# VectorE adds in place of adding DMAs in the first part of each FFN, and one group with three pairs in seven products instead of four

## The chip, the cores and the metric

The kernel runs on one core of a Trainium2 chip. The metric is the device time of one execution in microseconds. Three runs of the kernel before gave 2097.92, 2096.4 and 2097.1 us, median 2097.1. The profile is of one further execution.

## The reference

A trunk of two residual layers over 256 tokens of width 2048 in fp32. Each layer has a mixer (layer 0: sliding window attention beside a matrix memory; layer 1: forgetting attention) and an FFN of hidden width 5632. The change lies in the FFN:

```python
def swiglu(xn, w_gate, w_up, w_down):
    return (jax.nn.silu(xn @ w_gate) * (xn @ w_up)) @ w_down

# per layer, after the mixer
h = h + swiglu(rms_norm(h, norm_ffn[layer]), w_gate[layer], w_up[layer], w_down[layer])
```

## The kernel before

**Products.** An fp32 operand is split into a high and a low part in a reduced format: ScalarE casts the raw tile to `hi` (L187, L356), VectorE computes `lo = raw - hi` (L188, L357). A product of two split operands is three matmuls into one accumulator, hi·xh (L532), lo·xh (L533) and hi·xl (L534); the helper `three` issues them. The two token tiles of 128 are the stationary side, 512 columns of weights the moving side.

**Stages of an FFN.** The hidden width is cut into 11 groups of 512 columns, numbered 0 to 10, in three parts: groups 0 to 2, 3 to 6 and 7 to 10. Each part first does its groups (gate and up columns of the same number together, then SiLU and multiplication, then a turn of the result by DMA transposes on SyncE's queue and `join`, which splits it for the next product), and then two calls for `w_down`, each for 1024 output columns.

**Pairs of rows.** Every such call is a `pair_group` (L539). It walks over the contraction in pairs of 128 rows; a gate and up group has eight pairs. A plain pair (kind 0) does eight products, 24 matmuls. A mixed pair (kind 1) does seven products, 21 matmuls, after the scheme of Strassen and Winograd: `ra` and `rb` are two raw tiles of 128 x 2 x 512 (gate and up, or two column blocks of `w_down`), loaded by SyncE's DMA queue, 512 KB each. Sums of weight blocks are formed in place and split again:

1. `rb[:,0] += ra[:,0]`, before the change by a DMA that GpSimd issues: it reads those 256 KB of gate (or down) rows from HBM once more and adds them onto `rb` (L599).
2. `ra` is split (L187, L188), and the sum `rb` is split as `hu`, `lu` (L356, L357).
3. `rb[:,1] = rb[:,0] - rb[:,1]` on VectorE, 128x512 (L605), then `ra -= rb[:,1]`, 128x1024 (L607), and both results are split again (L356, L357).

`combine` (from L552) puts the products together after the last mixed pair.

**Which pairs are mixed.** `ORDER` makes three of eight pairs mixed (1, 3 and 5) and starts with a plain one; `HEAVY` makes four mixed (1, 3, 5, 7) and starts with a mixed one. `DENSE` lists the groups that take `HEAVY`. In the down products of the first part two of six pairs are mixed, in the other parts three of eight (`DOWN`).

**Order and buffers.** A scheduler fixes the order of each engine's stream when the kernel is built, and each engine then runs its stream in that order. Raw tiles of mixed pairs come from a pool of five buffers, those of plain pairs from another of four; a load can start when the instruction that last read its buffer is done. The `w_in_even` and `w_in_odd` projections use `pair_group` too, in a variant (`halves`) that has no adding DMA.

Of the kernel before, what the change touches and what calls it, by code (L numbers as in the profile page):

```python
# [12 lines left out]
ALU = mybir.AluOpType  # L13
# [10 lines left out]
NB = 512  # L24
# [11 lines left out]
ORDER = ((0, 0), (1, 1), (0, 2), (1, 3), (0, 4), (1, 5), (0, 6), (0, 7))  # L36
HEAVY = ((1, 1), (0, 0), (1, 3), (0, 2), (1, 5), (0, 4), (1, 7), (0, 6))
FOURTH = 7
DENSE = (1, 4, 5, 8, 9)
DOWN = {  # L40
    6: ((0, 0), (1, 1), (0, 2), (1, 3), (0, 4), (0, 5)),
    8: ((0, 0), (1, 1), (0, 2), (1, 3), (0, 4), (1, 5), (0, 6), (0, 7)),
# [33 lines left out]
def trunk(  # L76
# [19 lines left out]
    nc = tc.nc  # L96
# [58 lines left out]
    for n in (1, 2, 3):  # L155
# [8 lines left out]
        out=ident, in_=ident, pattern=[[-1, P]], compare_op=ALU.not_equal, fill=1.0, base=0, channel_multiplier=1  # L164
# [73 lines left out]
    sums = {}  # L238
# [116 lines left out]
    def split_plain(dst_h, dst_l, src):  # L355
        nc.scalar.copy(dst_h, src)  # L356
        nc.vector.tensor_tensor(out=dst_l, in0=src, in1=dst_h.bitcast(F32), op=ALU.subtract)  # L357
# [178 lines left out]
    def bank(par, name):  # L536
        return pm.tile([P, NB], F32, tag="pm", name=name) if par else pa.tile([P, NB], F32, tag="acc", name=name)

    def pair_group(fp, par, lhs, sums, mats, order, todo=(), halves=None, inner=None, raws=None):  # L539
        plain = [[bank(par, "acc") for _ in range(NT)] for _ in range(2)]  # L540
        begun = set()

        def fresh(*at):
            known = at in begun
            begun.add(at)
            return not known

        todo = list(todo)
        prods = None
        kinds = [kind for kind, _ in order]  # L550
        t0, t1 = slice(0, P), slice(P, 2 * P)

        def combine(prods):
            c = fp.tile([P, 4, NB], F32, tag="c", name="c", bufs=1)
            nc.scalar.copy(c[:, 0, :], prods[0])
            if halves is None:
                nc.vector.tensor_tensor(out=c[:, 1, :], in0=prods[3], in1=c[:, 0, :], op=ALU.add)
                nc.vector.tensor_tensor(out=c[:, 2, :], in0=prods[2], in1=c[:, 1, :], op=ALU.add)
                nc.vector.tensor_tensor(
                    out=c[:, 1:4:2, :],  # L560
                    in0=prods[1].rearrange("p (a n) -> p a n", a=1).broadcast_to([P, 2, NB]),
                    in1=c[:, 1:3, :],
                    op=ALU.subtract,
                )
                return c
            nc.vector.tensor_tensor(out=c[:, 2, :], in0=prods[3], in1=c[:, 0, :], op=ALU.add)
            nc.vector.tensor_tensor(out=c[:, 1, :], in0=prods[2], in1=c[:, 2, :], op=ALU.add)
            nc.vector.tensor_tensor(out=c[:, 3, :], in0=prods[1], in1=c[:, 1, :], op=ALU.subtract)
            nc.vector.tensor_tensor(out=c[:, 2, :], in0=prods[1], in1=c[:, 2, :], op=ALU.subtract)
            return c  # L570

        for pos, (kind, pair) in enumerate(order):
            k0 = 2 * pair
            if inner is not None and pos == len(order) - 1:
                c = combine(prods)
                inner()
            if not kind:
                last = pos == len(order) - 1
                walk = [(i, t) for i in range(CK) for t in range(NT)]
                if last:  # L580
                    walk.sort(key=lambda it: it[1])
                for m, (w, c0) in enumerate(mats):
                    hi, lo = load_chunk(w, k0, c0, NB)
                    run_due(todo, pos)
                    for i, t in walk:
                        ah, al = lhs(k0 + i)
                        ts = slice(t * P, (t + 1) * P)
                        three(
                            plain[m][t], ah[:, ts], al[:, ts], hi[:, i, :], lo[:, i, :],
                            fresh(m, t), last and i == CK - 1,  # L590
                        )
                continue
            first, last = 1 not in kinds[:pos], 1 not in kinds[pos + 1 :]
            if first:
                prods = [bank(1 - par, "prod") for _ in range(4)]
            ra, rb = (load_raw(w, k0, c0, NB, fp, W_RAWS if halves else RAWS, raws) for w, c0 in mats)
            if halves is None:
                (w, c0), part = mats[0], slice(k0 * P, (k0 + 1) * P)
                nc.gpsimd.dma_start(rb[:, 0, :], w[part, c0 : c0 + NB], accum_op=ALU.add)  # L599
            hg, lg = split_chunk(ra, NB)  # L600
            run_due(todo, pos)
            hu, lu = slot()
            if halves is None:
                split_plain(hu, lu, rb)
                nc.vector.tensor_tensor(out=rb[:, 1, :], in0=rb[:, 0, :], in1=rb[:, 1, :], op=ALU.subtract)  # L605
                both = rb[:, 1, :].rearrange("p (a n) -> p a n", a=1).broadcast_to([P, CK, NB])
                nc.vector.tensor_tensor(out=ra, in0=ra, in1=both, op=ALU.subtract)  # L607
                hc, lc = (a[:, 0, :] for a in slot())
                split_plain(hc, lc, rb[:, 1, :])
                hd, ld = slot()  # L610
                split_plain(hd, ld, ra)
                ht = [hu[:, 0, :], hd[:, 0, :], hc, hd[:, 1, :]]
                lt = [lu[:, 0, :], ld[:, 0, :], lc, ld[:, 1, :]]
            else:
                split_plain(hu[:, 1, :], lu[:, 1, :], rb[:, 1, :])
                nc.vector.tensor_tensor(out=ra[:, 0, :], in0=rb[:, 0, :], in1=ra[:, 0, :], op=ALU.add)
                nc.vector.tensor_tensor(out=rb[:, 0, :], in0=rb[:, 1, :], in1=rb[:, 0, :], op=ALU.subtract)
                nc.vector.tensor_tensor(out=rb[:, 1, :], in0=ra[:, 0, :], in1=rb[:, 1, :], op=ALU.subtract)
                nc.vector.tensor_tensor(out=ra[:, 1, :], in0=ra[:, 1, :], in1=rb[:, 1, :], op=ALU.subtract)
                parts = []  # L620
                for src in (ra, rb):
                    hs, ls = halves.pop(0)
                    halves.append((hs, ls))
                    split_plain(hs, ls, src)
                    parts.append((hs, ls))
                where = ((0, 0), (1, 0), (1, 1), (0, 1))
                ht = [parts[a][0][:, b, :] for a, b in where]
                lt = [parts[a][1][:, b, :] for a, b in where]
            sh, sl = sums(pair)
            xa, la = lhs(k0)  # L630
            xb, lb = lhs(k0 + 1)
            three(prods[0], xa[:, t0], la[:, t0], hg[:, 0, :], lg[:, 0, :], first, last)
            three(plain[0][0], xb[:, t0], lb[:, t0], hg[:, 1, :], lg[:, 1, :], fresh(0, 0), False)
            three(plain[1][0], sh[3], sl[3], hu[:, 1, :], lu[:, 1, :], fresh(1, 0), False)
            three(prods[1], sh[0], sl[0], ht[0], lt[0], first, last)
            three(prods[2], sh[2], sl[2], ht[1], lt[1], first, last)
            three(prods[3], sh[1], sl[1], ht[2], lt[2], first, last)
            three(plain[0][1], xb[:, t1], lb[:, t1], ht[3], lt[3], fresh(0, 1), False)
        if inner is None:
            c = combine(prods)  # L640
        return plain, c

    def ffn(layer, fp, sx, x4, sd, key, todo, idx_next=None, key_next=None, finish=None):
# [8 lines left out]
        for g0, g1 in zip(PARTS, PARTS[1:]):  # L652
            end = g1 == PARTS[-1]
            nk = 4 * (g1 - g0)
            order = DOWN[nk // 2]
            for g in range(g0, g1):
                par = (g1 - 1 - g) % 2
# [5 lines left out]
                    [(w_gate[layer], g * NB), (w_up[layer], g * NB)],  # L663
                    HEAVY if g in DENSE else ORDER,
                    todo,
                )
                todo = []
                for m in range(2):
# [79 lines left out]
            for n0 in (0, 2):  # L748
                if end and idx_next is None and n0 == 2:
                    for n in (2, 3):  # L750
                        acc = new_acc()
                        gemm(acc, m_of, wd, n * NB, NB, 0, nk, nk, skew=3 if n == 3 else 1, halved=n == 3)
                        close(acc, n)
                    continue
                plain, c = pair_group(
                    fp, 1 - n0 // 2, m_of, sums_d, [(wd, n0 * NB), (wd, (n0 + 1) * NB)], order, todo
                )
                todo = []
                if end and idx_next is None:
                    gf = fp.tile([P, D], F32, tag="c", name="gf", bufs=1)  # L760
                    nc.gpsimd.dma_start(gf, norm_final.partition_broadcast(P))
                for t in range(NT):
                    o = h[:, t, n0 * NB : (n0 + 2) * NB]
                    nc.vector.tensor_tensor(
                        out=o, in0=c[:, 2 * t : 2 * t + 2, :].rearrange("p a n -> p (a n)"), in1=o, op=ALU.add
                    )
                for m in range(2):
                    close(plain[m], n0 + m)
# [614 lines left out]
```

## Time and profile before

| | |
|---|---|
| median of three runs | 2097.1 us |
| profiled execution, its own time | 2095.33 us |
| its span, first to last instruction | 2093.6 us |
| matmuls on TensorE | 9443 |
| adding DMAs on GpSimd (L599) | 76 of 256 KB |
| first part of the FFN, layer 0 and 1 | from about 290 to 497 and from about 1360 to 1565 us of the span |

The page of the profile gives busy time by engine, a row of 40 slices, the chain of work that ended last, and groups of instructions. The trace itself answers closer questions: a windows view (busy time of each engine in a stretch of time), timelines of one engine with what ended each idle time, and lists of waits. PE is TensorE's matmuls, PEld its weight loads, DVE VectorE, ACT ScalarE, POOL GpSimd, SP SyncE. A row such as `lo<-raw,hi` names what an instruction writes and reads. Times in the timelines count from the start of the span.

### The profile page before, as it was taken

How to read it: one execution, taken by the hardware profiler on the slowest of the kernel's cores; microseconds unless marked ns; L12 is line 12 of the kernel's file. 1: busy time of each engine (PE TensorE's matmuls, PEld its weight loads, DVE VectorE, ACT ScalarE, POOL GpSimd, SP SyncE). 2: the span in 40 equal slices, each digit the busy share in tenths (PEclk: the TensorE clock that was granted, in tenths of full speed). 3: DMA queues.
4: the chain of work that ended last, by engine and by line, in shares of the span. 5: the costliest groups of instructions: out<-in, count | busy, mean ns of one | idle time of the engine just before them, and what ended most of it. 6: DMA issues, size and time to landing. Idle time of an engine off the chain costs nothing.

```text
span 2093.6 us, 27094 instructions
## 1 busy us (share of the span) xinstructions
PE 2072.1 (99%) x9443; PEld 1709.8 (82%) x9443; DVE 1794.4 (86%) x2217; ACT 1384.1 (66%) x1764; POOL 133.7 (6%) x171
## 2 busy tenths in 40 slices
PE   9999999999999999999999999999999999999998
PEld 8878887778888888888888888887788888888887
DVE  6788768988999998998899678578899999999995
ACT  6767677665567656667676776686655667557763
POOL 1010000000000000000000001000000000000000
PEclk9999999999999999999999999999999999999999
DMA  8666578777788777887676777597778777867864
GB/s 294 177 201 201 195 257 226 217 215 218 220 229 265 227 244 220 237 238 202 204 225 198 227 201 186 162 263 202 243 220 244 228 223 234 265 201 209 263 208 150
DMA packets 324698, 462.43 MB, mean 221 GB/s; under 512 B 108092, under 2 KB 116304, under 8 KB 324432
## 3 DMA queue, kind: packets, MB, share of 16 engines
q1 hardware_dynamic: 307088, 426.27, 64.8%
q0 software_dynamic: 16752, 33.33, 9.0%
q8 instruction: 74, 1.21, 0.2%
q10 hardware_dynamic: 720, 1.09, 0.1%
q14 instruction: 64, 0.52, 0.1%
HBM read 436.21 MB, written 2.12 MB: 209 GB/s over the span
## 4 chain that ended last, share of the span: by engine, by line
PE 75%; DVE 8%; DMA 6%; ACT 5%; issue 4%; SPq 0%; ACTq 0%; POOLq 0%; POOL 0%; DVEq 0%
PE acc L533 16%; PE acc L532 16%; PE acc L534 16%; PE prod L533 4%; PE prod L532 4%; PE prod L534 4%; PE acc L222 4%; PE acc L223 4%; PE acc L224 4%; DVE lo L188 2%; DVE lo L357 2%; DMA raw<-in_w_down_dram 2%; ACT hi L187 2%; DMA raw<-in_w_gate_dram 1%; ACT hi L356 1%
## 5 line engine op out<-in xcount | busy, mean ns | idle before, releaser
L188 DVE TENSOR_TENSOR lo<-raw,hi 128x1024 fp32r<-128x1024 f32 (+2 forms) x646 | 761.7, 1194 | 153.8 <-ACT hi L187 151.2
L187 ACT CAST hi<-raw 128x1024 fp32r<-128x1024 f32 (+2 forms) x646 | 651.6, 1026 | 319.8 <-PE acc L534 83.7
L533 PE MATMUL acc<-lo,xh 128*128 128x512 f32 x1260 | 491.7, 391 | 1.0 <-DVE lo L188 1.0
L534 PE MATMUL acc<-hi,xl 128*128 128x512 f32 x1260 | 490.1, 390 | 0.0
L532 PE MATMUL acc<-hi,xh 128*128 128x512 f32 x1260 | 478.6, 392 | 5.5 <-ACT hi L187 3.9
L356 ACT CAST hi<-raw 128x1024 fp32r<-128x1024 f32 (+1 forms) x329 | 291.4, 894 | 226.5 <-DVE raw L605 84.6
L357 DVE TENSOR_TENSOR lo<-raw,hi 128x1024 fp32r<-128x1024 f32 (+1 forms) x329 | 334.9, 1029 | 52.2 <-ACT hi L356 50.8
L532 PEld LDWEIGHTS acc<-hi,xh 128*128 128x128 f32 x1260 | 236.8, 188 | 58.8 <-ACT hi L187 7.7
L533 PEld LDWEIGHTS acc<-lo,xh 128*128 128x128 f32 x1260 | 236.8, 188 | 53.0 <-DVE lo L188 3.9
L534 PEld LDWEIGHTS acc<-hi,xl 128*128 128x128 f32 x1260 | 236.9, 188 | 48.9
L533 PE MATMUL acc<-lo,mh 128*128 128x512 f32 x466 | 181.6, 390 | 0.0
L534 PE MATMUL acc<-hi,ml 128*128 128x512 f32 x466 | 181.4, 389 | 0.0
L532 PE MATMUL acc<-hi,mh 128*128 128x512 f32 x466 | 175.8, 390 | 0.5 <-ACT hi L187 0.5
L607 DVE TENSOR_TENSOR raw<-raw 128x1024 f32<-128x1024 f32 x105 | 128.3, 1222 | 1.0
L599 POOL DMA_DIRECT2D raw<-in_w_gate_dram x76 | 65.1, 856 | 963.9 <-DMA raw<-in_w_up_dram 391.4
L223 PE MATMUL acc<-lo,mh 128*128 128x512 f32 (+1 forms) x322 | 126.3, 392 | 0.0
L222 PE MATMUL acc<-hi,mh 128*128 128x512 f32 (+1 forms) x322 | 125.8, 391 | 0.0
L224 PE MATMUL acc<-hi,ml 128*128 128x512 f32 (+1 forms) x322 | 123.7, 391 | 0.0
L532 PEld LDWEIGHTS acc<-hi,mh 128*128 128x128 f32 x466 | 87.5, 188 | 19.4 <-ACT hi L187 1.3
L533 PEld LDWEIGHTS acc<-lo,mh 128*128 128x128 f32 x466 | 87.5, 188 | 18.1
L534 PEld LDWEIGHTS acc<-hi,ml 128*128 128x128 f32 x466 | 87.5, 188 | 18.1
L223 PE MATMUL acc<-lo,xh 128*128 128x512 f32 (+3 forms) x288 | 99.7, 347 | 0.2 <-DVE lo L188 0.2
(361 smaller groups left out, 3093.3 us busy)
## 6 DMA issues: line engine op xcount, KB each, us to landing
raw<-in_w_gate_dram SPq DMA_DIRECT2D x176, 512.0 KB, 5.2
raw<-in_w_up_dram SPq DMA_DIRECT2D x176, 512.0 KB, 5.4
raw<-in_w_down_dram SPq DMA_DIRECT2D x176, 512.0 KB, 5.7
raw<-in_w_in_odd_dram SPq DMA_DIRECT2D x88, 512.0 KB, 5.3
raw<-in_w_in_even_dram SPq DMA_DIRECT2D x51, 512.0 KB, 4.8
raw<-in_w_gate_dram POOLq DMA_DIRECT2D x76, 256.0 KB, 5.7
raw<-in_w_out_even_dram SPq DMA_DIRECT2D x32, 512.0 KB, 5.4
raw<-in_w_out_odd_dram SPq DMA_DIRECT2D x32, 512.0 KB, 4.8
```

Of the source, the lines that this page charges most:

```text
L187: latest[0] = nc.scalar.copy(hi[:, k, 0:n], raw[:, k, 0:n])
L188: nc.vector.tensor_tensor(out=lo[:, k, 0:n], in0=raw[:, k, 0:n], in1=hi[:, k, 0:n].bitcast(F32), op=ALU.subtract)
L222: nc.tensor.matmul(o, ah[:, ts], hi, start=(k == 0), stop=False)
L223: nc.tensor.matmul(o, ah[:, ts], lo, start=False, stop=False)
L224: nc.tensor.matmul(o, al[:, ts], hi, start=False, stop=(k == k_all - 1 and cs.stop == n))
L356: nc.scalar.copy(dst_h, src)
L357: nc.vector.tensor_tensor(out=dst_l, in0=src, in1=dst_h.bitcast(F32), op=ALU.subtract)
L532: nc.tensor.matmul(o, ah, hi, start=start, stop=False)
L533: nc.tensor.matmul(o, ah, lo, start=False, stop=False)
L534: nc.tensor.matmul(o, al, hi, start=False, stop=stop)
L599: nc.gpsimd.dma_start(rb[:, 0, :], w[part, c0 : c0 + NB], accum_op=ALU.add)
L607: nc.vector.tensor_tensor(out=ra, in0=ra, in1=both, op=ALU.subtract)
```

## The change

`ADDING = 3` is new. Both FFN calls of `pair_group` pass `adding=g0 >= ADDING`, where `g0` is the first group of a part, so it is false in the first part (`g0` is 0) and true in the second and third (3 and 7). Where it is true, GpSimd's DMA adds as before; where it is false, a VectorE instruction adds `ra[:,0]` onto `rb[:,0]`, 128x512, ahead of the split of `rb`. Beside that, group 1 leaves `DENSE`, so that it takes `ORDER`.

```diff
-DENSE = (1, 4, 5, 8, 9)
+DENSE = (4, 5, 8, 9)
+ADDING = 3
...
-    def pair_group(fp, par, lhs, sums, mats, order, todo=(), halves=None, inner=None, raws=None):
+    def pair_group(fp, par, lhs, sums, mats, order, todo=(), halves=None, inner=None, raws=None, adding=False):
...
             ra, rb = (load_raw(w, k0, c0, NB, fp, W_RAWS if halves else RAWS, raws) for w, c0 in mats)
-            if halves is None:
+            if adding:
                 (w, c0), part = mats[0], slice(k0 * P, (k0 + 1) * P)
                 nc.gpsimd.dma_start(rb[:, 0, :], w[part, c0 : c0 + NB], accum_op=ALU.add)
             hg, lg = split_chunk(ra, NB)
             run_due(todo, pos)
             hu, lu = slot()
             if halves is None:
+                if not adding:
+                    nc.vector.tensor_tensor(out=rb[:, 0, :], in0=ra[:, 0, :], in1=rb[:, 0, :], op=ALU.add)
                 split_plain(hu, lu, rb)
...
                     HEAVY if g in DENSE else ORDER,
                     todo,
+                    adding=g0 >= ADDING,
...
-                    fp, 1 - n0 // 2, m_of, sums_d, [(wd, n0 * NB), (wd, (n0 + 1) * NB)], order, todo
+                    fp, 1 - n0 // 2, m_of, sums_d, [(wd, n0 * NB), (wd, (n0 + 1) * NB)], order, todo, adding=g0 >= ADDING
```

In the changed kernel the lines from here on stand one to four higher: the DMA is L600, the VectorE add L606, the subtractions L608 and L610, the `lo` splits L189 and L358.

Where the change moves instructions, three places. First GpSimd's stream, from the norms ahead of the first FFN on; each row is an instruction with its tiles and a count of equal ones. Before:

```order
L1108 TENSOR_TENSOR st<-st,mhalf 128x2 x4
L599 DMA raw<-in_w_gate_dram 128x512 x3
L254 TENSOR_TENSOR r<-tot,mhalf 128x2
L599 DMA raw<-in_w_gate_dram 128x512 x7
L599 DMA raw<-in_w_down_dram 128x512 x4
L599 DMA raw<-in_w_gate_dram 128x512 x14
L599 DMA raw<-in_w_down_dram 128x512 x6
```

In the changed kernel:

```order
L1112 TENSOR_TENSOR st<-st,mhalf 128x2 x4
L255 TENSOR_TENSOR r<-tot,mhalf 128x2
L600 DMA raw<-in_w_gate_dram 128x512 x14
L600 DMA raw<-in_w_down_dram 128x512 x6
L600 DMA raw<-in_w_gate_dram 128x512 x14
```

The ten adding DMAs of groups 0 to 2 and the four of the first part's down products are gone; the second part's 14 and 6 stay.

Second, VectorE's stream at the end of group 0 of layer 0, where the splits of the coming pairs stand among the splits of the normalised input (`xl`, `s`, `sx`). Before:

```order
L357 TENSOR_TENSOR lo<-raw,hi 128x1024 x2
L362 SCALAR_TENSOR_TENSOR xl<-box,gT,xh 128x256 x4
L357 TENSOR_TENSOR sx_2411<-s_3243,sx_2410 128x512
L605 TENSOR_TENSOR raw<-raw 128x512
L188 TENSOR_TENSOR lo<-raw,hi 128x1024
L272 TENSOR_TENSOR s_3331<-full 128x128
L274 TENSOR_TENSOR s_3331<-full 128x128
L607 TENSOR_TENSOR raw<-raw 128x1024
```

In the changed kernel:

```order
L358 TENSOR_TENSOR lo<-raw,hi 128x1024 x2
L363 SCALAR_TENSOR_TENSOR xl<-box,gT,xh 128x256 x4
L606 TENSOR_TENSOR raw<-raw 128x512
L358 TENSOR_TENSOR sx_2411<-s_3242,sx_2410 128x512
L608 TENSOR_TENSOR raw<-raw 128x512
L189 TENSOR_TENSOR lo<-raw,hi 128x1024
L273 TENSOR_TENSOR s_3330<-full 128x128
L275 TENSOR_TENSOR s_3330<-full 128x128
```

The new add (L606) stands between `xl` and `sx`, ahead of the subtraction of another pair.

Third, VectorE's stream in group 1 of the changed kernel, around the add of the sixth mixed pair; numbers behind the names tell the buffers' tiles apart. Its pair is `raw_3630` (gate) and `raw_3632` (up).

```order
L610 TENSOR_TENSOR raw_3494<-raw_3494,raw_3496 128x1024
L358 TENSOR_TENSOR lo_3099<-raw_3496,hi_3098 128x512
L679 SCALAR_TENSOR_TENSOR c_3433<-c_3433,r_3113 128x512
L358 TENSOR_TENSOR lo_3109<-raw_3564,hi_3108 128x1024
L358 TENSOR_TENSOR lo_3101<-raw_3494,hi_3100 128x1024
L608 TENSOR_TENSOR raw_3564<-raw_3564 128x512
L606 TENSOR_TENSOR raw_3632<-raw_3630,raw_3632 128x512
L610 TENSOR_TENSOR raw_3562<-raw_3562,raw_3564 128x1024
```

And SyncE's stream of the loads there:

```order
L135 DMA raw_3630<-in_w_gate_dram 128x2x512
L135 DMA raw_3614<-in_w_up_dram 128x2x512
L135 DMA raw_3666<-in_w_gate_dram 128x2x512
L135 DMA raw_3693<-in_w_up_dram 128x2x512
L135 DMA raw_3632<-in_w_up_dram 128x2x512
```

The place of `raw_3632` is that of `raw_3496`, which the `lo_3099` split above reads last; before the change no VectorE instruction read a loaded tile before ScalarE's cast of it had.

## The prediction

> **What bounds the kernel now.** I start with busy time and the chain that ended last.
>
> ```profile
> PE 2072.1 (99%) x9443; PEld 1709.8 (82%) x9443; DVE 1794.4 (86%) x2217; ACT 1384.1 (66%) x1764; POOL 133.7 (6%) x171
> PE 75%; DVE 8%; DMA 6%; ACT 5%; issue 4%; SPq 0%; ACTq 0%; POOLq 0%; POOL 0%; DVEq 0%
> ```
>
> TensorE sets the end, but only on average, so the question is where it stands still. A busy share cannot tell, because matmul ends are modelled. Counting can: in the timeline, 55 start-to-start intervals lie between these two matmuls of an undisturbed stretch.
>
> ```profile
> 321.69 0.39 PE L224 MATMUL acc<-hi,ml 128*128 128x512 f32 x1
> 334.16 0.39 PE L532 MATMUL acc<-hi,xh 128*128 128x512 f32 x1
> ```
>
> So one matmul takes (334.16 − 321.69) / 55 = 0.2267 us. The windows view gives, after the length, busy time and count of each engine, then clock, DMA share and GB/s. Here are both FFNs: group 0; its end and early group 1; groups 1 and 2; the two down products; then, for layer 0, the gate and up groups of the second part and a piece of them.
>
> ```profile
> 290.00:340.00 50.00, 50.00 (x222) 41.43 (x221) 35.03 (x53) 38.80 (x55) 3.36 (x4) 1.00 0.93 279
> 340.00:385.00 45.00, 41.80 (x170) 31.37 (x170) 39.75 (x52) 29.44 (x39) 3.46 (x4) 0.99 0.67 194
> 385.00:427.00 42.00, 42.00 (x182) 34.69 (x181) 38.83 (x45) 26.75 (x30) 2.56 (x3) 0.97 0.87 248
> 427.00:497.00 70.00, 68.58 (x301) 55.23 (x301) 64.45 (x72) 44.75 (x50) 3.54 (x5) 1.00 0.75 225
> 497.00:745.00 248.00, 248.00 (x1096) 205.43 (x1095) 229.98 (x251) 157.85 (x173) 16.95 (x20) 1.00 0.78 231
> 620.00:662.00 42.00, 42.00 (x187) 34.80 (x186) 39.83 (x46) 29.26 (x33) 2.56 (x3) 1.00 0.91 254
> 1408.00:1453.00 45.00, 41.73 (x171) 31.08 (x170) 40.10 (x53) 29.79 (x39) 3.42 (x4) 1.00 0.66 194
> 1453.00:1495.00 42.00, 41.67 (x184) 34.21 (x184) 37.84 (x44) 25.63 (x29) 2.58 (x3) 1.00 0.90 249
> 1495.00:1565.00 70.00, 67.97 (x292) 54.51 (x291) 64.06 (x72) 44.98 (x50) 3.42 (x4) 0.98 0.74 222
> ```
>
> Length less count × 0.2267 is lost time: 6.5, 0.7 and 1.8 us in the rows from 340, and 6.2, 0.3 and 3.8 us in those from 1408: 19.3 us in all. The row 497:745, four groups with products and adding DMAs, loses nothing (1096 × 0.2267 = 248.5). Only the first part has stalls to give back. Finer windows at the stalls:
>
> ```profile
> 350.00:353.40 3.40, 2.58 (x9) 1.28 (x8) 3.40 (x7) 3.40 (x5) 0.43 (x1) 1.00 0.64 129
> 369.40:372.40 3.00, 1.99 (x6) 0.88 (x6) 3.00 (x5) 2.92 (x4) 0.00 (x0) 1.00 0.37 82
> 380.50:383.90 3.40, 2.03 (x7) 0.95 (x6) 2.19 (x2) 3.27 (x4) 0.77 (x1) 1.00 0.37 140
> 383.90:387.30 3.40, 3.40 (x9) 2.69 (x9) 3.40 (x5) 3.40 (x5) 0.09 (x1) 0.50 0.69 95
> 429.00:433.00 4.00, 3.14 (x13) 1.85 (x11) 3.67 (x4) 4.00 (x6) 0.00 (x0) 1.00 0.22 44
> 1418.00:1421.00 3.00, 2.18 (x7) 0.97 (x6) 3.00 (x6) 3.00 (x5) 0.00 (x0) 1.00 0.89 184
> 1437.00:1440.40 3.40, 1.93 (x6) 1.02 (x6) 3.40 (x5) 3.13 (x4) 0.00 (x0) 1.00 0.39 93
> 1447.50:1455.00 7.50, 6.58 (x25) 3.93 (x24) 6.29 (x7) 7.37 (x8) 0.84 (x1) 1.00 0.55 114
> 1496.70:1500.10 3.40, 1.54 (x5) 0.61 (x4) 2.98 (x4) 3.40 (x5) 0.00 (x0) 1.00 0.19 39
> 1500.10:1503.50 3.40, 3.40 (x7) 2.21 (x8) 3.40 (x4) 3.40 (x5) 0.00 (x0) 0.50 0.48 97
> ```
>
> By the same count, group 1 loses 1.6 + 1.8 + 1.4 (369.4 to 387.3) and 2.0 + 1.8 (from 1437): 8.6 us. The start of the down products loses 1.1 (429) and 2.3 + 1.8 (from 1496.7): 5.2 us. The end of group 0 loses 1.4 (350) and 1.4 (1418): 2.8 us. In the last two VectorE and ScalarE are busy throughout, so no DMA is to blame there. What stands ahead of the others is in the timelines of ScalarE and of GpSimd (in brackets: idle time before the instruction and what ended it):
>
> ```profile
> 365.37 1.57 ACT L356 CAST hi<-raw 128x1024 fp32r<-128x1024 f32 x2 [5.27 <-DMA raw<-in_w_gate_dram]
> 428.25 1.05 ACT L356 CAST hi<-raw 128x1024 fp32r<-128x1024 f32 x1 [5.84 <-DMA raw<-in_w_gate_dram]
> 1433.18 1.57 ACT L356 CAST hi<-raw 128x1024 fp32r<-128x1024 f32 x2 [5.73 <-DMA raw<-in_w_gate_dram]
> 1496.04 1.05 ACT L356 CAST hi<-raw 128x1024 fp32r<-128x1024 f32 x1 [7.35 <-PE acc L534]
> ```
>
> ```profile
> 360.10 0.84 POOL L599 DMA_DIRECT2D raw<-in_w_gate_dram  x1 [9.67 <-DVE lo L357]
> 423.41 0.85 POOL L599 DMA_DIRECT2D raw<-in_w_gate_dram  x1 [16.26 <-DVE c L675]
> 1428.21 0.84 POOL L599 DMA_DIRECT2D raw<-in_w_gate_dram  x1 [11.00 <-DVE xl L357]
> 1491.49 0.88 POOL L599 DMA_DIRECT2D raw<-in_w_gate_dram  x1 [17.31 <-DVE lo L357]
> ```
>
> Each cast starts 4.6 to 5.3 us after an adding DMA was issued, and ScalarE stands still for 5.3 to 7.4 us. The fourth wait is labelled with TensorE, but the add was issued 4.55 us before the cast starts, so I read it as the same wait. ScalarE's stop starves VectorE's subtractions (its own waits behind the first two casts, below), and TensorE runs out of split weights about 4 us after the cast's start, or at once.
>
> ```profile
> 366.45 1.23 DVE L357 TENSOR_TENSOR lo<-raw,hi 128x1024 fp32r<-128x1024 f32 x1 [2.89 <-ACT hi L356]
> 429.33 1.23 DVE L357 TENSOR_TENSOR lo<-raw,hi 128x1024 fp32r<-128x1024 f32 x1 [4.14 <-ACT hi L356]
> ```
>
> **The change, part by part.** Each of the two FFNs swaps 13 adding DMAs of its first part for VectorE adds: nine in groups 0, 1 and 2, four in the down products. One mixed pair of group 1 turns plain, which takes a 14th adding DMA away.
>
> *TensorE.* One product more per layer, three matmuls: 6 × 0.2267 = **+1.4 us**, with nothing to hide it.
>
> *Start of the down products.* The ScalarE wait goes. In its place stands an add on VectorE. Its price follows from neighbours in VectorE's timeline that run back to back:
>
> ```profile
> 348.77 0.69 DVE L605 TENSOR_TENSOR raw<-raw 128x512 f32<-128x512 f32 x1
> 349.37 1.23 DVE L188 TENSOR_TENSOR lo<-raw,hi 128x1024 fp32r<-128x1024 f32 x1
> 350.50 0.29 DVE L272 TENSOR_TENSOR s<-full 128x128 f32<-128x128 f32 x1
> ```
>
> A 128x512 add takes 349.37 − 348.77 = 0.60 us, a 128x1024 one 1.13 us. I take the loss as gone: **−5.2 us** (bounds 0 and −5.2).
>
> *Group 1.* Its two stalls go with the wait, unless VectorE takes its place. A mixed pair costs VectorE 4 × 1.13 + 2 × 0.60 = 5.7 us for splits and subtractions of weights; a plain pair 2 × 1.13 = 2.3. So group 1 saves 3.4 and pays 3 × 0.60: 1.6 us less work. But it inherits the backlog of group 0, whose end is VectorE's. I let 2.6 us of the 8.6 stay: **−6.0 us** (bounds 0 and −8.6).
>
> *End of group 0.* Rows 350 and 1418 show VectorE full. The third add must wait for its weights to land, and the fourth falls into the backlog: with 0.60 and some waiting, 1.0 us per layer, **+2.0 us**. Row 290:340 leaves 15 idle us on VectorE ahead of it, enough to take all adds of group 0: bound 0. The other bound is three adds and about one wait of 0.9 per layer, +5.4.
>
> *New waits.* The add needs both raw tiles, so VectorE, not GpSimd's queue, now waits for the loads. By the order of the changed kernel the load of the 6th pair's second tile is released by the last lo split of the pair before; four VectorE instructions stand between that and its add, a 128x512 multiply, two 128x1024 and a 128x512: 2 × 0.60 + 2 × 1.13, about 3.5 us. Loads of 340 to 427, SyncE's view:
>
> ```profile
> DMA to landing us min/median/max: 3.6/4.8/8.8
> ```
>
> So this add waits 0.1 to 5.3 us, by the median 1.3. Behind it on VectorE stand the subtractions and lo splits of that pair and the next, which TensorE needs; on SyncE's queue later loads come behind a load that waits for a tile. Six of a layer's late adds stand alike (6th, 7th, 9th, 10th, 12th, 13th). What such waits cost the end lies between 0, where they only replace waits for ScalarE, and 6 × 5.3 per layer. I take **+1.0 us** for both layers, near the lower end: in row 620 VectorE is busy 39.83 of 42 (95%), and TensorE loses nothing (187 × 0.2267 = 42.4), so waits elsewhere give way.
>
> The sum: 1.4 − 5.2 − 6.0 + 2.0 + 1.0 = −6.8 us. The profiled run took 2095.3 us (span 2093.6 and 1.7 around it), 1.8 under the median of 2097.1: 2088.5 against its own time, **2090.3** on the runs' median.
>
> A check from VectorE's side: in 340 to 497 it is busy 39.75 + 38.83 + 64.45 = 143.0 of 157, so it waits 14.0, half of it (2.89 + 4.14) in the two waits above. Ten of the 13 adds lie here: + 6.0 − 3.4 = 145.6. TensorE needs 656 × 0.2267 = 148.7. At row 620's 95% VectorE takes 145.6 / 0.948 = 153.6; my sum, 3.4 less per layer, gives 157 − 3.4 = 153.6 too. So VectorE becomes the bound of this stretch, and 8.0 us of waits are granted to it.
>
> *GpSimd and the DMA queues.* 28 adding DMAs of 256 KB go. GpSimd is busy 3.5 of 45 us in row 340; nothing is gained there: 0, as the only ones that waited were the casts above.
>
> A place where a page bears on a term: rows 383.9 and 1500.1 show a granted clock of 0.50. The longest TensorE wait before the first is this:
>
> ```profile
> 381.73 0.50 PE L532 MATMUL prod<-hi,sx 128*128 128x512 f32 x1 [0.92 <-ACT hi L356]
> ```
>
> The Trainium skill, "TensorE: Matmul & The Clock Gate", section "HAM oscillation — how this bites in real kernels", ties the halved clock to idle gaps of TensorE longer than about 3.4 us. By that rule, rows 383.9 and 1500.1 would not be half clock; this trace shows them after many short gaps, so the measurement decides, and their 1.4 + 1.8 us stay in the terms above.
>
> **Rivals.**
>
> *VectorE takes the wait over (same).* VectorE is the bound of the stretch anyhow, by the check. If the six late adds wait about half of the median's 1.3 us, 3.4 to 4.4 us per layer, and the waits for ScalarE stay, the stretch takes 157 as before: 2097.1. For it: the lead is counted in VectorE's own instructions, so its backlog does not lengthen it. Against it: row 620.
>
> *The DMA was not to blame (same).* Row 350 stalls without it, and group 1's stalls could be that backlog, met again. Then only TensorE's matmuls and a little remain: 2098.5. Against it: ScalarE's own wait names the DMA, and 429 lies far from any backlog.
>
> *VectorE stuck behind landings (slower).* One mechanism: adds wait, in order, for loads that their buffers release too late. If the six adds wait the median's 1.3 us and the 7.0 us of other waits stay, the stretch takes 145.6 + 7.0 + 7.8 = 160.4, 3.4 us per layer more than now: 2103.9. If they wait halfway to the longest, 3.3 us each, and the others vanish in these, 145.6 + 19.8 = 165.4: 2113.9. I take 2105, near the median's. It decides from 157 − 145.6 = 11.4 us of waits in all on VectorE in this stretch, and shows from 13.5. Against it: now VectorE waits 7.0 there without the adding DMAs, and a landing at 3.6 costs nothing. The same Trainium skill page, section "Architectural detail: the array is 16× 32×32, not 1× 128×128", states that VectorE works strictly first in, first out; by that rule ready work can't pass a waiting add, which is this rival's condition.
>
> *A clean first part (faster still).* If all 19.3 us go, 2097.1 − 19.3 + 1.4 = 2079.2.
>
> **How the numbers follow.** A measurement of this kernel can tell about 0.2%, 4.2 us: faster is below 2092.9, slower above 2101.3. Forecast (2086.7 to 2092.9) 0.46; cleaner still, 0.10; VectorE takes it over 0.18; DMA not to blame 0.06; slower 0.20. So faster 0.56, same 0.24, slower 0.20. The likeliest case by itself spans 2086.7 to 2092.9: at 2086.7 group 1 gives back all of its 8.6 and the new waits cost nothing. The range 2083 to 2103 reaches down past halfway between the forecast and the clean case, and up to the near end of the slower one; it leaves out about 0.05 below and 0.15 above.
>
> **What would show it.** Right: no ScalarE wait over 3 us behind a DMA at the start of group 1 and of the down products; the windows there lose under 1 us; no half clock near 384 and 1500; matmuls 9449. VectorE's adds of the first part show idle time before them that a landing ended: up to 1 us each by the forecast, over 2 by the slower rival. Wrong: if the stalls return with VectorE's adds as releaser, or if TensorE still waits at the same places with ScalarE never idle.

## The result and the profile after

The changed kernel takes 2087.8 us (median of six runs, 2086.12 to 2089.62) against 2096.18 us for the kernel before in the same comparison. The ratio is 0.9956 with a 95% interval of 0.9945 to 0.9967. That is 8.4 us less by the medians, where −6.8 had been forecast. The time lies in the range, and on the side that had the larger chance. Why is another matter: the sum was close because two of its terms were wrong in opposite ways, which is luck, and the remedy on which it was built turned out to be only one of two.

The head of the page after, and its chain of waits by engine:

```profile
span 2084.4 us, 26995 instructions
PE 2066.4 (99%) x9449; PEld 1713.1 (82%) x9449; DVE 1804.5 (87%) x2235; ACT 1383.7 (66%) x1760; POOL 113.2 (5%) x143
PE 86%; DMA 4%; DVE 4%; ACT 4%; issue 3%; SPq 0%; ACTq 0%; POOLq 0%; POOL 0%; DVEq 0%
```

TensorE's share of the chain has gone from 75 to 86%: less of the end is set by somebody else. The matmuls are the 9449 expected. GpSimd's instructions fell from 171 to 143, which are the 28 adding DMAs; the trace before has 105 of them, 76 of `w_gate` and 29 of `w_down` (the table ahead counts those of `w_gate` alone). The stages of the two first parts, in the windows view as before:

```profile
340.00:385.00 45.00, 42.59 (x174) 34.36 (x174) 40.54 (x54) 29.58 (x38) 0.00 (x0) 0.92 0.58 184
385.00:427.00 42.00, 42.00 (x187) 34.80 (x186) 39.41 (x47) 27.48 (x30) 0.00 (x0) 1.00 0.68 217
427.00:497.00 70.00, 67.93 (x301) 55.56 (x301) 67.31 (x77) 41.95 (x48) 0.95 (x1) 1.00 0.67 212
1408.00:1453.00 45.00, 44.15 (x194) 35.92 (x193) 44.47 (x59) 33.38 (x40) 0.00 (x0) 1.00 0.69 219
1453.00:1495.00 42.00, 42.00 (x187) 34.79 (x186) 38.73 (x45) 26.90 (x31) 0.00 (x0) 1.00 0.62 190
1495.00:1565.00 70.00, 67.61 (x294) 55.15 (x293) 65.03 (x75) 39.37 (x45) 0.91 (x1) 0.98 0.67 214
```

In layer 1 the row from 1408 holds 194 matmuls where it held 171. In layer 0 the row from 340 holds 174 instead of 170, at a clock of 0.92, and the down products (rows 427 and 1495) hold 301 and 294 as against 301 and 292: the down products gained nothing. The places where the kernel before stood still, and two new ones, in finer windows:

```profile
352.90:356.30 3.40, 1.19 (x5) 0.33 (x3) 3.40 (x5) 0.90 (x1) 0.00 (x0) 0.93 0.90 286
356.30:361.90 5.60, 5.41 (x13) 4.30 (x14) 5.60 (x9) 3.59 (x6) 0.00 (x0) 0.50 0.96 341
369.40:372.40 3.00, 3.00 (x15) 2.48 (x14) 2.97 (x5) 1.59 (x3) 0.00 (x0) 1.00 0.56 175
380.50:383.90 3.40, 3.40 (x17) 2.82 (x16) 3.06 (x5) 2.12 (x4) 0.00 (x0) 1.00 0.75 217
429.00:433.00 4.00, 4.00 (x20) 3.30 (x19) 4.00 (x6) 3.17 (x5) 0.00 (x0) 1.00 0.53 100
1437.00:1440.40 3.40, 3.40 (x17) 2.81 (x16) 3.40 (x5) 2.78 (x3) 0.00 (x0) 1.00 0.49 151
1447.50:1455.00 7.50, 7.50 (x35) 6.20 (x34) 7.50 (x12) 7.50 (x9) 0.00 (x0) 1.00 0.99 364
1496.70:1500.10 3.40, 3.40 (x17) 2.81 (x15) 3.12 (x5) 2.99 (x4) 0.00 (x0) 1.00 1.03 389
1526.00:1537.00 11.00, 8.61 (x33) 6.61 (x32) 9.63 (x11) 7.99 (x10) 0.00 (x0) 0.84 0.75 233
```

Every stall that the prediction put down to an adding DMA is gone: 15 matmuls in 369.4 to 372.4 where there were 6, 17 in 1496.7 to 1500.1 where there were 5. In their place stand a longer end of group 0 in layer 0, with the half clock behind it (6.8 us, of which the row above shows 5.6), and a stop late in the down products of both layers. This is TensorE's timeline behind these stops, one in each layer:

```profile
473.11 0.49 PE L533 MATMUL acc<-hi,mh 128*128 128x512 f32 x1 [2.04 <-ACT hi L357]
```

```profile
1531.68 0.49 PE L533 MATMUL acc<-hi,mh 128*128 128x512 f32 x1 [2.39 <-ACT hi L357]
```

Going back from the first: ScalarE, in order, had stood before the cast of a plain tile of `w_down` until it landed (ScalarE's timeline); its load had been issued at 466.91 (SyncE's), right after VectorE was done with the `lo` split of another plain tile (VectorE's):

```profile
470.58 1.04 ACT L188 CAST hi<-raw 128x1024 fp32r<-128x1024 f32 x1 [2.02 <-DMA raw<-in_w_down_dram]
```

```profile
466.91 0.37 SPq L135 DMA_DIRECT2D raw<-in_w_down_dram  x1
```

```profile
465.66 1.23 DVE L189 TENSOR_TENSOR lo<-raw,hi 128x1024 fp32r<-128x1024 f32 x1
```

So the new stop is a late release of a raw tile by VectorE. It is not the wait that the prediction feared: VectorE's waits for landings before the new adds, as its list of waits gives them for layer 0 (us in total, times, longest us), are small.

```profile
DVE raw L606 <- DMA raw<-in_w_up_dram: 0.5, 2, 0.3
DVE raw L606 <- DMA raw<-in_w_down_dram: 0.5, 1, 0.5
```

Matching the same matmul in both traces shows where the 9.2 us of the two spans (2093.6 − 2084.4) come from. Layer 0's first part gives 1.5 us (a matmul near 300 stands 0.45 us later than before, one near 500 1.00 us earlier), layer 1's gives 5.9 us (3.30 earlier near 1360, 9.18 near 1570). The other 2.3 us lie between: 0.8 at 865, and 1.5 from 1000 on, where layer 1 begins. The code is the same there, but the scheduler has put a few instructions in another order (five matmuls near 1020 us, for one).

### The profile page after: what moved, and what is told of

The parts are those of the page before. It is cut to its first block, busy times and chain, and to the rows that moved or that the text cites. A ratio compares the mean times of both kernels' runs of the same rounds, so it can differ in the third digit from the quotient of the medians.

```text
span 2084.4 us, 26995 instructions
## 1 busy us (share of the span) xinstructions
PE 2066.4 (99%) x9449; PEld 1713.1 (82%) x9449; DVE 1804.5 (87%) x2235; ACT 1383.7 (66%) x1760; POOL 113.2 (5%) x143
## 4 chain that ended last, share of the span: by engine, by line
PE 86%; DMA 4%; DVE 4%; ACT 4%; issue 3%; SPq 0%; ACTq 0%; POOLq 0%; POOL 0%; DVEq 0%
PE acc L533 19%; PE acc L534 19%; PE acc L535 19%; PE prod L533 5%; PE prod L534 5%; PE prod L535 5%; PE acc L224 4%; PE acc L223 4%; PE acc L225 4%; DVE lo L189 1%; DMA raw<-in_w_down_dram 1%; ACT hi L188 1%; DMA raw<-in_w_gate_dram 1%; PE p L387 1%; ACT box L323 1%
## 5 line engine op out<-in xcount | busy, mean ns | idle before, releaser
L189 DVE TENSOR_TENSOR lo<-raw,hi 128x1024 fp32r<-128x1024 f32 (+3 forms) x648 | 762.7, 1192 | 148.5 <-ACT hi L188 146.2
L188 ACT CAST hi<-raw 128x1024 fp32r<-128x1024 f32 (+3 forms) x648 | 654.0, 1027 | 352.9 <-PE acc L535 130.1
L357 ACT CAST hi<-raw 128x1024 fp32r<-128x1024 f32 (+1 forms) x323 | 286.9, 894 | 193.7 <-DVE raw L608 78.2
L358 DVE TENSOR_TENSOR lo<-raw,hi 128x1024 fp32r<-128x1024 f32 (+1 forms) x323 | 328.3, 1026 | 31.2 <-ACT hi L357 30.4
L610 DVE TENSOR_TENSOR raw<-raw 128x1024 f32<-128x1024 f32 x103 | 125.6, 1220 | 0.9
L225 PE MATMUL acc<-hi,xl 128*128 128x512 f32 (+3 forms) x288 | 98.8, 344 | 0.0
```

The lines of the kernel that those rows point to most:

```text
L188: latest[0] = nc.scalar.copy(hi[:, k, 0:n], raw[:, k, 0:n])
L189: nc.vector.tensor_tensor(out=lo[:, k, 0:n], in0=raw[:, k, 0:n], in1=hi[:, k, 0:n].bitcast(F32), op=ALU.subtract)
L225: nc.tensor.matmul(o, al[:, ts], hi, start=False, stop=(k == k_all - 1 and cs.stop == n))
```

## The experiments

All times are medians of at least five runs. Each ratio is to the kernel before on the same chip, whose medians in these comparisons were 2095.3 to 2096.4 us. The first four take the change apart.

**The dense groups alone.** Against the changed kernel:

```diff
-ADDING = 3
+ADDING = 0
```

> Only group 1 leaves the dense groups; every weight sum is still formed by an adding DMA. Theory (the gain came from ScalarE's waits for adding DMAs): the waits stay, at the start of the down products wholly (5.2 us lost), in group 1 in part, since its first mixed pair now follows a plain pair; six matmuls more cost 1.4. Time 1 to 4 us under the kernel before, about 2093, and ScalarE still shows waits of over 4 us behind adding DMAs. Rival (the gain came from the lighter group 1 on VectorE, 3.4 us per layer): nearly all of the measured 8.4 us is here, 2088 to 2089.

Measured: 2079.72 us, ratio 0.9923 (0.9911 to 0.9936). Both theories are beaten, and the prediction's is beaten badly: without one VectorE add, moving group 1 to three mixed pairs brings 16.7 us, twice what the whole change brings. The windows of this kernel's layer 0, then the adding DMA of group 1's second mixed pair (the fifth of the layer's `w_gate` adds, of which group 0 has three) with its time to landing, and two casts of ScalarE:

```profile
360.00:372.00 12.00, 12.00 (x54) 9.94 (x54) 10.85 (x15) 7.16 (x9) 0.85 (x1) 1.00 0.61 199
380.00:388.00 8.00, 8.00 (x37) 6.64 (x36) 5.19 (x6) 6.62 (x8) 0.88 (x1) 1.00 0.63 124
427.00:433.00 6.00, 6.00 (x28) 4.98 (x27) 5.66 (x7) 4.75 (x6) 0.00 (x0) 1.00 0.81 255
461.00:470.00 9.00, 9.00 (x46) 7.45 (x45) 5.51 (x7) 5.62 (x8) 0.85 (x1) 1.00 0.59 183
```

```profile
360.80 0.85 POOL L600 DMA_DIRECT2D raw<-in_w_gate_dram  x1 [9.35 <-DVE c L558]
DMA to landing us min/median/max: 6.0/6.0/6.0
```

```profile
364.59 1.05 ACT L357 CAST hi<-raw 128x1024 fp32r<-128x1024 f32 x1 [4.47 <-issue]
374.11 1.06 ACT L357 CAST hi<-raw 128x1024 fp32r<-128x1024 f32 x1 [0.32 <-PE acc L535]
```

The adding DMA is issued at 360.80, as late as before (360.10), and lands at 366.8. Before, ScalarE's stream had come to the cast of this sum while the add was still under way: the cast at 365.37, after 5.27 us of standing, which held up the casts and the SiLU behind it. Here the cast of the sum is the one at 374.11, 7 us behind the landing, with other work of the stream ahead of it. (The cast at 364.59 is that of the first mixed pair, whose add had landed at 354.8; what ended its 4.47 us the profile doesn't tell, but it was no adding DMA.)

54 matmuls run in 12 us, one per 0.222 us, the full pace: TensorE loses nothing. The same holds for the other stalls. The kernel before has six waits of ScalarE of 3.3 to 7.4 us that end with the landing of a `w_gate` add, four in group 1 (also at 380.63 and 1447.63) and two in group 2, and a stall of TensorE at each. Here two such waits are left, 1.4 and 1.3 us long, with no stall. So the chain from the adding DMA over ScalarE to TensorE was read rightly, but the wait could go without a single add being moved.

**The adds alone.**

```diff
-DENSE = (4, 5, 8, 9)
+DENSE = (1, 4, 5, 8, 9)
```

> Only the adds move to VectorE in the first part; group 1 keeps four mixed pairs. Theory: ScalarE's waits for adding DMAs are gone, so group 1 (9.9 us lost before by exact count) gains most of it, and 1.4 us of matmuls are saved against the changed kernel, but VectorE has 3.4 us and one add more per layer: 2087 to 2092. Rival (lighter group 1 made the gain): VectorE is now more loaded than in either kernel, 2095 or more.

Measured: 2085.13 us, ratio 0.9946 (0.9932 to 0.9959), within the theory's range. So the adds do remove the stalls by themselves, even with a mixed pair at the start of group 1: its window 364 to 395 holds 138 matmuls in 31 us. Either part helps alone (−16.7 and −11.3 us by the medians), and both together help least (−8.4; the intervals of the last two overlap).

**VectorE adds in the gate and up groups only, and in the down products only.** Each against the changed kernel:

```diff
-... order, todo, adding=g0 >= ADDING
+... order, todo, adding=True
```

> The changed kernel with adding DMAs again in all down products, VectorE adds only in the gate and up groups 0 to 2. Theory: the stalls at the start of the first down products (5.2 us in both layers) come back, the new ones late in them (3.4 us and their half clock) go: 0 to 2 us over the changed kernel, 2088 to 2090. Rival (each VectorE add is a burden that the scheduler must hide): faster than the changed kernel by 2 to 5 us.

Measured: 2084.26 us, ratio 0.9942 (0.9929 to 0.9954): 3.5 us under the changed kernel, the rival's result. The stalls at the start of the down products don't come back, but this edit could not bring them back: the add in front of them (423.41 before) reads `w_gate` and is that of group 2's last mixed pair, which VectorE does here too.

```diff
-                    adding=g0 >= ADDING,
+                    adding=True,
```

> The changed kernel with adding DMAs again in groups 0 to 2, VectorE adds only in the down products of the first part. Theory: as the kernel with only the dense groups changed, with the down products' stalls exchanged for the new ones: within 2 us of it, about 2092. Rival (the down products made the gain): 2088 or less.

Measured: 2079.59 us, ratio 0.992 (0.9908 to 0.9933). It is within 0.2 us of the dense groups alone, as the theory had it relative to them; the number 2092 fell with the first run. Four VectorE adds in the down products by themselves cost nothing measurable, and with adding DMAs in group 2 again the stop at 429 stays away.

**What it is about group 1.** The prediction's story (adding DMAs are slow) is not enough as it stood. `HEAVY` differs from `ORDER` in two things, a mixed pair at the start (lead) and a fourth one (load). Both kernels here have adding DMAs everywhere (`ADDING = 0`), and group 1 takes an order of its own:

```diff
+GROUP1 = ((0, 0), (1, 1), (0, 2), (1, 3), (1, 5), (0, 4), (1, 7), (0, 6))
```

> Adding DMAs everywhere and four mixed pairs in group 1 as in the kernel before, but group 1 starts with a plain pair. Theory of lead (the stalls of group 1 and of the down products came from a mixed pair at the start of group 1, whose adding DMA had no plain pair ahead of it to cover it): stalls gone as with three mixed pairs, and 1.4 us of matmuls fewer: 2077 to 2081. Rival, theory of load (3.4 us of VectorE work more per layer in group 1): stalls come back, 2087 to 2096.

Measured: 2089.42 us, ratio 0.9972 (0.9961 to 0.9983).

```diff
+GROUP1 = ((1, 1), (0, 0), (1, 3), (0, 2), (1, 5), (0, 4), (0, 6), (0, 7))
```

> Adding DMAs everywhere and three mixed pairs in group 1, but group 1 starts with a mixed one. Theory of lead: the stalls of group 1 come back, about as in the kernel before, 2087 to 2096. Theory of load: as with the dense groups alone, 2079 to 2082.

Measured: 2090.51 us, ratio 0.9977 (0.9968 to 0.9985). Each alone brings back 10 to 11 of the 16.7 us, so neither theory has all of it: each names a piece, at different places. Windows with the fourth mixed pair (e5), at the start and at the end of group 1 and late in the down products:

```profile
364.00:395.00 31.00, 31.00 (x139) 25.66 (x138) 28.90 (x35) 22.40 (x25) 1.73 (x2) 1.00 0.70 195
399.50:410.00 10.50, 7.82 (x24) 5.18 (x23) 9.23 (x11) 4.93 (x6) 0.00 (x0) 0.85 0.84 249
472.00:476.00 4.00, 2.72 (x11) 1.63 (x10) 3.56 (x5) 2.65 (x5) 0.00 (x0) 1.00 0.76 219
```

The adding DMA of group 2's first mixed pair and ScalarE's cast of its sum, in the same kernel:

```profile
397.95 0.85 POOL L601 DMA_DIRECT2D raw<-in_w_gate_dram  x1 [5.56 <-DMA raw<-in_w_up_dram]
403.57 1.04 ACT L358 CAST hi<-raw 128x1024 fp32r<-128x1024 f32 x1 [1.66 <-DMA raw<-in_w_gate_dram]
```

And with the mixed pair at the start (e6), with ScalarE's cast behind the adding DMA:

```profile
369.10:372.10 3.00, 2.02 (x7) 0.92 (x6) 3.00 (x5) 3.00 (x4) 0.00 (x0) 1.00 0.34 72
380.00:387.30 7.30, 6.37 (x24) 3.75 (x23) 6.58 (x7) 7.30 (x9) 0.86 (x1) 1.00 0.52 122
427.00:433.00 6.00, 6.00 (x28) 4.99 (x27) 5.92 (x6) 4.10 (x5) 0.00 (x0) 1.00 0.54 98
```

```profile
365.18 1.57 ACT L358 CAST hi<-raw 128x1024 fp32r<-128x1024 f32 x2 [5.24 <-DMA raw<-in_w_gate_dram]
```

With the mixed pair first, the kernel before is there again at the start of group 1: the same wait of 5.24 us (5.27 before), the same stops at 369 and 380. With the plain pair first these are gone (139 matmuls in 31 us), but with the fourth mixed pair TensorE stops at 400 to 407, at the turn to group 2. That is an adding DMA again: ScalarE waits for its landing, GpSimd had waited for the landing of the raw tile that it adds to, and that tile's load had been issued only at 392.49, when VectorE's split of an earlier tile had freed its buffer. Layer 1 has the same stop with a wait of 3.34 us, until 1473.75. The order of this run also puts two mixed pairs next to each other, (1, 3) and (1, 5), so it doesn't tell the fourth pair's work from that place. The stop at 429, which lies behind the adding DMA of group 2's last mixed pair, is in neither: it needs both.

**Which VectorE adds cost.** All with three mixed pairs in group 1; `adding` is false only where named. Group 0 (`adding=g > 0`), then group 2 (`adding=g != 2`), down products with adding DMAs:

> VectorE adds in group 0 only, adding DMAs in groups 1 and 2 and all down products, group 1 with three mixed pairs. Theory (VectorE adds cost where VectorE has no spare time, and ahead of 335 us it has some): 2077 to 2081, with no stall late in the down products. Rival (any VectorE add in the gate and up groups of the first part lengthens the end of group 0 and halves the clock behind it): 2083 to 2085.

Measured: 2078.39 us, ratio 0.9913 (0.99 to 0.9927), as the theory had it.

> VectorE adds in group 2 only, adding DMAs in groups 0 and 1 and all down products, group 1 with three mixed pairs. Theory (the adds of group 2 put VectorE behind, a plain raw tile of the first down products is freed late, its load and ScalarE's cast come late): the stall near 470 and 1530 us of 1.4 us and more in each layer is back, 2081 to 2084. Rival: the backlog comes from groups 0 and 1 as well, so group 2 alone shows none of it, 2079 to 2080.

Measured: 2079.42 us, ratio 0.9923 (0.9911 to 0.9935); the rival was right here. Then group 1 alone (`adding=g != 1`), all but group 1 (`adding=g0 >= ADDING or g == 1`, VectorE in the down products), and groups 1 and 2:

> VectorE adds in group 1 only, adding DMAs elsewhere, three mixed pairs in group 1. The dense groups alone gave 2079.7, the whole change 2087.8. Theory A (the adds of group 1 themselves cost: VectorE is still behind there from group 0): 2083 to 2087, with a stall late in the down products. Theory B (no single group costs; the backlog of all 13 adds adds up until a plain raw tile is freed too late): 2078 to 2081.

Measured: 2081.25 us, ratio 0.9928 (0.9915 to 0.994), 0.3 over theory B and under A.

> The changed kernel with adding DMAs again in group 1 only: VectorE adds in groups 0 and 2 and in the first part's down products. Theory A: the cost goes, 2078 to 2081. Theory B: ten of 13 adds are still there, seven of them one after the other from group 2 on, so about half of the cost stays: 2082 to 2086.

Measured: 2082.94 us, ratio 0.9939 (0.9926 to 0.9951), as theory B had it.

> VectorE adds in groups 1 and 2, adding DMAs in group 0 and all down products, three mixed pairs in group 1. Theory A: as with group 1 alone. Theory B: six adds in a row put VectorE about 3 us further behind than the dense groups alone by the end of group 2, so the stall late in the down products is back although neither group shows it alone: 2081 to 2085.

Measured: 2081.89 us, ratio 0.9931 (0.9918 to 0.9945); B's time, but its stall late in the down products isn't in the profile, whose loss lies at the end of group 0. Ordered by the number of VectorE adds per layer, with three mixed pairs in group 1:

| adds | where | us |
|---|---|---|
| 0 | none | 2079.7 |
| 3 | group 0 / 1 / 2 | 2078.4 / 2081.3 / 2079.4 |
| 4 | down products | 2079.6 |
| 6 | groups 1, 2 | 2081.9 |
| 9 | groups 0, 1, 2 | 2084.3 |
| 10 | groups 0, 2, down products | 2082.9 |
| 13 | the change | 2087.8 |

Up to four adds are within some 1.5 us of none, about the spread of one kernel's runs; nine and more cost 3 to 8 us. No single place is guilty, the cost adds up. The stop late in the down products shows it best: counted from start to start, TensorE loses there 3.0, 3.1 and 4.5 us in both layers together with nine, ten and 13 adds, and at most 0.8 with six or fewer. The piece of the down products ahead of it, in the changed kernel:

```profile
461.00:470.00 9.00, 9.00 (x42) 7.42 (x41) 8.89 (x11) 3.78 (x4) 0.00 (x0) 1.00 0.53 181
```

VectorE is busy 8.89 of 9 us, where with the dense groups alone (row 461 above) it has caught up and is busy 5.51. This share alone doesn't decide it: with ten adds VectorE is busy 6.92 there, and the stop comes as well.

**Group 1 with VectorE adds and four mixed pairs, a mixed one first.** Against the kernel of group 1 alone:

```diff
-DENSE = (4, 5, 8, 9)
+DENSE = (1, 4, 5, 8, 9)
```

> The kernel before with VectorE adds in group 1 alone: group 1 keeps its four mixed pairs and starts with a mixed one, adding DMAs everywhere else. Theory of lead alone: the stall at the start of group 1 goes with its wait for the adding DMA, about 7 us of the 9.9 lost there, 2085 to 2089. Theory of load beside it (four mixed pairs plus four adds put VectorE 5.8 us per layer behind the dense groups alone): the stalls move to the end of group 1 and to the down products, 2088 to 2094. If neither, the stall at the start stays and the time is that of the kernel before.

Measured: 2095.96 us, ratio 1.0 (0.9991 to 1.0009). The start of group 1 and the end of group 2, then ScalarE:

```profile
364.00:395.00 31.00, 31.00 (x138) 25.43 (x137) 30.99 (x37) 23.01 (x25) 0.00 (x0) 1.00 0.60 178
425.00:431.00 6.00, 3.99 (x14) 2.20 (x13) 5.58 (x6) 6.00 (x8) 0.00 (x0) 1.00 0.32 66
```

```profile
424.34 1.05 ACT L357 CAST hi<-raw 128x1024 fp32r<-128x1024 f32 x1 [4.33 <-DMA raw<-in_w_gate_dram]
```

The stall at the start of group 1 is gone, as lead alone has it, and VectorE pays with 30.99 busy us of 31. The loss comes back at later places, the largest at the adding DMA of group 2's last mixed pair (cast at 424.34, 14 matmuls in 6 us; in layer 1 the cast at 1492.23 after a wait of 7.79 us, with the half clock behind it). That is the theory of load, more strongly than its 2088 to 2094.

**A version that beats both.** The fastest measured is VectorE adds in group 0 only (2078.39 us), 9.4 us under the changed kernel; the dense groups alone are within the noise of it. Both leave the end of group 0, where TensorE lost 3.3 us in layer 0 in the kernel of the dense groups alone.

## Why the prediction was right, and where it was not

**TensorE, +1.4.** Right: six matmuls more.

**Group 1, −6.0.** The stalls gave 10.1 us (counted from start to start: 5.6 in layer 0 and 4.5 in layer 1, now 0), more than the upper bound of 8.6, since a row of the windows view also counts matmuls that only overlap its edges, one or two too many in each row. That the stalls go with the wait held: in the kernel before and in the three variants of group 1 that keep such stalls (plain pair first, mixed pair first, VectorE adds with four mixed pairs) the largest stalls of groups 1 and 2 lie behind a cast that waited for the landing of an add, and where these waits are gone, so are these stalls. That also answers the rival "the DMA was not to blame". What failed is the remedy: the wait was taken to go only with its DMA. Three fewer matmuls' worth of saving per layer bought a mixed pair that cost much more. The step that failed is the one on the mixed pair: it was priced at 1.6 us of VectorE work and nothing for its place in the order. Measured alone, with every adding DMA in place, it takes these waits away and is worth 16.7 us.

**Start of the down products, −5.2.** The place was misread: the stop belongs to group 2's last mixed pair, whose add is the tenth of the layer's `w_gate` adds. The old stop is gone, but rows 427 and 1495 hold about as many matmuls as before: the new one late in them took the gain back (8.2 us lost in the two rows before, 7.4 after). The rival "VectorE takes the wait over" was right in this stage, by another path than its landings.

**End of group 0, +2.0.** Layer 0 lost 2.1 us before and 5.8 now (2.6 of it half clock), layer 1 2.9 and 1.4: +2.2 in all. The size is right. That the VectorE adds of group 0 do it is shown in part. In layer 0 the four kernels with these adds and three mixed pairs in group 1 have a wait of ScalarE of 2.9 to 3.3 us for the load of a plain `w_gate` tile in front of this stop, and the other kernels that start group 1 with a plain pair have 1.0 to 1.8 us. But with VectorE adds in groups 1 and 2 alone the half clock comes as well, and in layer 1 the kernel with group 0's adds alone loses less than the one with none (1.2 against 2.8 us).

**New waits, +1.0.** The waits for landings before layer 0's adds are 1.0 us in all in the two rows above, and 0.7 in layer 1, far under the median's 1.3 us each (another 1.3 us in layer 0, with no releaser named, fall into VectorE's idle time ahead of 335); loads were early enough. The slower rival's mechanism (adds stuck behind landings) therefore never began. What the adds cost came by their own 0.60 us and by what they push back: beside the dense groups' change they cost 8.1 us (2087.8 against 2079.7), where these two steps had +3.0 in all.

**The sum.** Group 1 gave 4 us more than its term and the start of the down products 4 us less, so the two errors cancelled. With the six matmuls, the first parts give −10.1 − 0.8 + 2.2 + 1.4 = −7.3 us. The rest of the 9.2 us between the spans lies where no term stood: −2.3 behind the first part of layer 0 and +0.4 ahead of it.

**The check from VectorE's side** held in its number: 145.6 us of work were forecast for 340 to 497, and 40.54 + 39.41 + 67.31 = 147.3 are there. It said that VectorE becomes the bound of this stretch. Taken at its word it also said that adding work to VectorE there, and not taking a DMA away, is what the time turns on.

**The clean case** (2079.2, chance 0.10) is about what the dense groups alone measure. It was reached by the half of the change that the prediction had as an afterthought.

## What to carry to other kernels

A wait that ends a stall's chain names what was waited for, but not the only way to be rid of it: ask why the engine came to it so early, and what could stand ahead of it in the order. An adding DMA that took about 5 to 6 us to land cost group 1 of a layer 5 us of TensorE time or nothing, by the order of its pairs. Where two parts of a change treat the same stall, price each alone and both together: here either removed it, and the second one's cost was all that it added. An engine that is busy 95% of a stage may still take a few instructions more (four adds in the down products cost nothing measurable, with VectorE busy 67.66 of 70 us), but their cost adds up, and it shows later and elsewhere, here as buffers freed late, loads behind them and casts behind those.

## What the runs showed of the hardware

Away from the end of the runs, the granted clock fell to 0.50 twelve times in the 14 traces, each time behind a stretch in which TensorE had worked but little. The longest single wait of TensorE there is 1.72 us at the change's first fall and 2.75 us at any of the twelve. Each fall lasted 3.41 us, or in one case (layer 0 of the change) 6.83 us, and in each trace they lie on a fixed grid. In the kernel before they begin at 383.92 and 1500.08, which is 327 times 3.4133 us apart, and in the changed kernel at 355.81 and 1533.40, 345 times 3.4133 us apart.

Counting the matmuls that start in each step of this grid, of which there are 15 at full pace, tells when the clock falls. Behind a step at full clock with five or fewer it fell in seven cases of seven, with six in four of seven, with seven in one of eleven, and with eight or more never. So what counts here is not one wait but how much of one step the waits take, and with it where they lie on the grid. The change's stop at the end of group 0 in layer 0 falls into one step, 352.39 to 355.81, with five matmuls; that of the dense groups alone, drawn out from 351.8 to 357.2, leaves eight in its emptiest step, and their clock doesn't fall.

The half clock cost the change about 4 us in its profiled execution, 2.6 in layer 0 and the rest in layer 1. The mean clock of all six of its runs, 0.996 to 0.997 against 0.998 to 0.999 with the dense groups alone, says that it is no accident of one run. It is part of why the change stands so far above its halves.
